# An encoder layer in four passes: the parts of the MLP's weights stored by the first pass, w_down summed over two groups, and POOL's elementwise work moved to VectorE

## The chip, the core and the metric

The kernel runs on one core of one Trainium2 chip. The metric is the device time of one execution in microseconds (us); the median of several executions is compared. The core's engines are named as in the profile: PE is TensorE (the matrix engine, with its weight loads listed apart as PEld), DVE is VectorE, ACT is ScalarE, POOL is GpSimd, and SP is SyncE, whose queue issues most of the DMAs. Each engine takes its instructions in a fixed order and waits by semaphores for the others. SBUF is the memory on the chip in which tiles live, PSUM the eight banks into which PE accumulates.

## What is computed

One layer of a bidirectional encoder on 2048 tokens of width 1024, in float32:

```python
h = x
y = rmsnorm(h, norm_mix_g) @ w_in                     # 1024 -> 2560: q, k, v, conv input and gate
att  = dilated_sliding_attention(rot(q), rot(k), v)   # 8 heads of 64; three window patterns, summed by their softmax weights
conv = silu(layernorm(depthwise_conv31(a * sigmoid(g)) + conv_b))   # 512 channels
h = h + concat([att, conv]) @ w_out                   # 1024 -> 1024
xq = rmsnorm(h, norm_x_g) @ w_xq                      # cross attention: 4 heads of 256, 256 memory rows
h = h + softmax(xq @ xk.T / 16) @ xv @ w_xo
u = rmsnorm(h, norm_mlp_g) @ w_up                     # 1024 -> 4096
h = h + square(relu(u)) @ w_down                      # 4096 -> 1024
out = rmsnorm(h, norm_final_g)
```

## The kernel before

**Numbers in two parts.** PE multiplies float16. Each float32 operand is scaled by a power of two and held as a high part (the value rounded to float16) and a low part (what the rounding left). A product takes three matmuls into the same PSUM tile, high by high, high by low and low by high: `mm3`, lines L369 to L371. A weight tile comes from memory as float32 (`raw`, 512 KB) and is split on the chip by `split_to`: ACT writes the high part (L356) and DVE the low part (L357), each over 128 x 1024 elements.

**Passes.** The front (the projections, the memory's keys and values, the far parts of the attention) takes about the first 680 us. Behind it the tokens are taken in four passes of 512, by `post(p)` (L1464 on): the out-projection (`o`, 8 weight tiles), the cross attention's scores (`xs`, whose weights are the products `ascr` made earlier) and its output (`x`, from `bscr`), the MLP (L1548 to L1586) and the final norm and output (L1589 to L1607). Each of these reads weights through `wpost` (L1322): a DMA of SP into one of three `raw` buffers, then the split into a `ws` buffer. There are four of these, two in the pool `wp` and two in `wq`, and `turn_w` deals them out, two tiles to the one pool and two to the other. So every weight is loaded and split in every pass.

**The MLP of passes 0 to 2.** It runs over eight groups (`fg`) of 512 hidden columns. In a group, four w_up tiles give four PSUM tiles `up` of 24 matmuls of 512 columns each, in the three PSUM banks of kind "mm"; DVE reads each with the norm's scale and the relu (L1564, `rl`), ACT squares and rounds it (L1565, L1566) and DVE takes the low part (L1567). The parts of four tiles (`hh`) lie in a buffer that is one of two (`xquad`). Then four w_down tiles of 256 columns give eight PSUM tiles `dn` of 12 matmuls, and DVE adds each to the residual rows (L1580). The norm's scale comes from a chain that starts where the cross attention ends: PE sums the squares over the partitions (`nps`, L1417), DVE scales (L338, `st_v`), POOL takes the power −1/2 (L342), DVE refines it (L343 to L345), PE spreads it over the partitions (`nrb`, L350), and ACT copies it with a scale (L1545).

**The last pass.** `last_mlp` (L1609) computes its w_down products with seven products where eight stand in the plain form, from sums and differences of quarters of w_down (`quarter`, `sums`) which `piece` splits on the chip (L1691); its `hidden` (L1635) reads w_up through `wpost` as the other passes do.

**Work woven in.** While pass p runs, two generators are advanced by `weave` (L93): the attention of pass p + 1 at 0.95 steps per step of `post`, and its convolution at 0.6. A convolution unit is 31 steps on DVE (L384 and L386, `cacc`); `conv_ln` (L392) norms it over the channels, and at its end POOL scales (L440), ACT rounds (L441) and POOL takes the low part (L442). The attention's inner loop writes scores `s` (L1228), DVE applies the mask and takes the maximum (L1010, `sm`), ACT takes the exponential (L1011), PE transposes (L1017, `pt`), ACT and DVE split (L1020, L1021), PE multiplies by v (L1025 to L1027, `opt`). `combine` (L1121) sums the three patterns of a pair of heads with their softmax weights; its elementwise work is on POOL (`W`), but for the last pair of pass 0.

**What sets the order.** The program is written as these generators. A planner, which simulates the timeline, then fixes each engine's order of instructions; `tc.issue_after` (in `after`) keeps some instructions behind a named one. Tiles of a pool with one tag share buffers, and a new tile waits until the one before it is no longer used.

## Time and profile before

| | |
|---|---|
| median of 3 runs | 2701.1 us (2698.41 to 2701.16) |
| the profiled execution | 2705.9 us |
| its span, first to last instruction | 2704.0 us |
| granted PE clock, mean over the span | 0.994 |
| PE busy | 2645.2 us (98%) |
| DVE busy | 2048.3 us (76%) |
| ACT busy | 1314.5 us (49%) |
| POOL busy | 349.7 us (13%) |
| MLP of pass 0, of pass 1, of pass 2 | 837 to 1209, 1355 to 1726, 1872 to 2241 us |
| DMA | 413.79 MB, mean 153 GB/s |

All rows but the first describe one profiled execution. A row of the timeline reads: start and duration in us, the engine, the line of the kernel, the operation, output <- inputs, shapes, and xN where N like instructions stand in one row; in brackets the idle time of the engine just before it and the instruction that ended it. A row of groups ends with the busy time and the mean ns of one instruction, then the idle time before the group's instructions and what ended most of it. A matmul's recorded duration reaches past the start of the next one, since matmuls are pipelined: the distance of the starts is its cost in a stream. Idle time of an engine that nobody waits for costs nothing.

### The profile page before, as it was taken

The page shows a single profiled execution, that of the slowest core. Times are in us where ns is not written, and L with a number is a line of the kernel's source. Part 1 is how long each engine was busy: PE and PEld are TensorE (multiplying, and loading weights), DVE is VectorE, ACT ScalarE, POOL GpSimd, SP SyncE. Part 2 cuts the span into 40 slices and gives each one's busy share as a digit, 9 for nine tenths or more (in the row PEclk, how much of TensorE's full clock was granted, in tenths as well). Part 3 has the DMA queues.
Part 4 walks back from the last instruction along what each step waited for, and adds up shares of the span by engine and source line. Part 5 has one row for each costly group of instructions (what it writes and reads, how often), then busy time and mean ns, then how long its engine had stood idle before and what let it go on. Part 6 is the DMA issues. An engine that isn't in the chain of part 4 may idle for free.

```text
span 2704.0 us, 41123 instructions
## 1 busy us (share of the span) xinstructions
PE 2645.2 (98%) x15514; PEld 1446.8 (54%) x15514; DVE 2048.3 (76%) x3713; ACT 1314.5 (49%) x2189; POOL 349.7 (13%) x405
## 2 busy tenths in 40 slices
PE   8999999999899999999999999999999999999998
PEld 7844448777454455445545554455445545444443
DVE  5887656567798887667988866689887656679997
ACT  5737554476454344535544344455434434445543
POOL 1144002032001011300011013000110310000000
PEclk9999999999999999999999999999999999999999
DMA  9977968565635444544444545434444445223341
GB/s 270 297 258 215 286 223 266 167 191 163 168 92 134 125 132 124 150 137 150 121 118 124 140 114 164 156 113 125 125 129 129 138 131 179 94 86 102 95 124 63
DMA packets 497702, 413.79 MB, mean 153 GB/s; under 512 B 86525, under 2 KB 432561, under 8 KB 496736
## 3 DMA queue, kind: packets, MB, share of 16 engines
q1 hardware_dynamic: 490096, 396.14, 50.1%
q10 hardware_dynamic: 5184, 9.01, 0.9%
q0 software_dynamic: 2224, 6.01, 0.6%
q8 instruction: 122, 2.00, 0.3%
q14 instruction: 76, 0.62, 0.1%
HBM read 342.52 MB, written 68.57 MB: 152 GB/s over the span
## 4 chain that ended last, share of the span: by engine, by line
PE 79%; DVE 9%; DMA 5%; issue 3%; POOL 2%; ACT 1%; SPq 0%; DVEq 0%; POOLq 0%; ACTq 0%
PE dn L369 7%; PE dn L371 7%; PE dn L370 7%; PE up L369 7%; PE up L370 7%; PE up L371 7%; PE lin L371 3%; PE lin L369 3%; PE lin L370 3%; PE pt L1017 2%; PE xs L369 2%; PE xs L371 2%; PE xs L370 2%; PE o L369 2%; PE o L371 2%
## 5 line engine op out<-in xcount | busy, mean ns | idle before, releaser
L369 PE MATMUL up<-mh,ws_u 128*128 128x512 f16 x1024 | 389.5, 381 | 0.6 <-ACT mh L1457 0.6
L370 PE MATMUL up<-ml,ws_u 128*128 128x512 f16 x1024 | 389.6, 381 | 0.0
L371 PE MATMUL up<-mh,ws_u 128*128 128x512 f16 x1024 | 388.6, 380 | 0.0
L386 DVE SCALAR_TENSOR_TENSOR cacc<-cu,cw,cacc 128x512 f32<-128x512 f32 x480 | 367.6, 766 | 5.0
L371 PE MATMUL dn<-hhh,ws_d 128*128 128x512 f16 x768 | 290.5, 379 | 0.0
L370 PE MATMUL dn<-hhl,ws_d 128*128 128x512 f16 x768 | 290.5, 379 | 0.0
L369 PE MATMUL dn<-hhh,ws_d 128*128 128x512 f16 x768 | 283.1, 379 | 0.9 <-DVE h L1580 0.9
L356 ACT ACTIVATE ws_u<-raw_u,bd 128x1024 f16<-128x1024 f32 x128 | 146.7, 1146 | 237.6 <-PE dn L371 186.9
L356 ACT ACTIVATE ws_d<-raw_d,bd 128x1024 f16<-128x1024 f32 x100 | 114.8, 1148 | 280.2 <-PE up L371 252.4
L1580 DVE SCALAR_TENSOR_TENSOR h<-dn,bd,h 128x512 f32<-128x512 f32 x192 | 140.8, 746 | 62.8 <-PE dn L371 60.1
L357 DVE SCALAR_TENSOR_TENSOR ws_u<-raw_u,bd,ws_u 128x1024 f16<-128x1024 f32 x128 | 164.0, 1282 | 18.5 <-ACT ws_u L356 16.9
L1010 DVE CUSTOM_DVE_ANT_0 sm<-s,mask,qks 128x256 f32<-128x256 f32 (+1 forms) x384 | 150.9, 434 | 29.5 <-PE s L1228 21.6
L371 PEld LDWEIGHTS <-ws_u 128*128 128x128 f16 x1024 | 100.5, 98 | 120.7 <-issue 1.8
L1564 DVE SCALAR_TENSOR_TENSOR rl<-up,ssumx 128x512 f32<-128x512 f32 x96 | 65.7, 690 | 129.5 <-PE up L371 129.3
L369 PEld LDWEIGHTS <-ws_u 128*128 128x128 f16 x1024 | 100.7, 98 | 114.9 <-issue 1.8
L370 PEld LDWEIGHTS <-ws_u 128*128 128x128 f16 x1024 | 101.0, 99 | 113.7 <-issue 1.8
L357 DVE SCALAR_TENSOR_TENSOR ws_d<-raw_d,bd,ws_d 128x1024 f16<-128x1024 f32 x100 | 133.0, 1330 | 30.1 <-ACT ws_d L356 29.5
L1011 ACT ACTIVATE sm<-sm,o 128x256 f32<-128x256 f32 (+1 forms) x288 | 116.3, 453 | 69.9 <-DVE o L1010 69.1
L1021 DVE TENSOR_TENSOR pl<-pt,ph 128x512 f16<-128x512 f32 x160 | 109.4, 685 | 36.5 <-ACT ph L1020 36.3
L371 PEld LDWEIGHTS <-ws_d 128*128 128x128 f16 x768 | 75.1, 98 | 89.2
L1020 ACT CAST ph<-pt 128x512 f16<-128x512 f32 x160 | 91.2, 572 | 60.8 <-PE pt L1017 60.8
L342 POOL TENSOR_TENSOR nr<-st_v,mhalf 128x4 f32<-128x4 f32 (+1 forms) x15 | 13.4, 895 | 825.8 <-DVE st_v L338 825.8
(497 smaller groups left out, 6436.8 us busy)
## 6 DMA issues: line engine op xcount, KB each, us to landing
raw_u<-in_w_up_dram SPq DMA_DIRECT2D x128, 512.0 KB
raw_d<-in_w_down_dram SPq DMA_DIRECT2D x100, 512.0 KB
scan<-in_w_up_dram SPq DMA_DIRECT2D x32, 512.0 KB
scan<-in_w_down_dram SPq DMA_DIRECT2D x32, 512.0 KB
raw_o<-in_w_out_dram SPq DMA_DIRECT2D x32, 512.0 KB
raw_a<-ascr SPq DMA_DIRECT2D x32, 512.0 KB
raw_b<-bscr SPq DMA_DIRECT2D x32, 512.0 KB
b<-in_w_down_dram SPq DMA_DIRECT2D x28, 512.0 KB
```

Of the source, the lines that this page charges most:

```text
L356: ACT.activation(t[:, 0], raw, AF.Copy, scale=scale)
L357: DVE.scalar_tensor_tensor(t[:, 1], raw, scale, t[:, 0], op0=ALU.mult, op1=ALU.subtract)
L369: PE.matmul(o, lh, rh, start=first, stop=False, skip_group_check=more)
L370: PE.matmul(o, lh, rl, start=False, stop=False, skip_group_check=more)
L371: last["pe"] = PE.matmul(o, ll, rh, start=False, stop=end, skip_group_check=more)
L386: DVE.scalar_tensor_tensor(acc, u[:, t:t + 512], cw[:, c, t:t + 1], acc, op0=ALU.mult, op1=ALU.add)
L1010: last["dve"] = DVE.tensor_tensor_reduce(dst, so, mask[:, 256 * m:256 * m + nk], SCORE, 3e38, ALU.add, ALU.min, mn)
L1011: last["act"] = ACT.activation(dst, dst, AF.Exp, bias=mn, scale=-1.0)
L1020: ACT.copy(ph, pt)
L1021: DVE.tensor_tensor(pl, pt, ph, op=ALU.subtract)
L1564: last["dve"] = DVE.scalar_tensor_tensor(r, pt, 0.0, rsb, op0=ALU.max, op1=ALU.mult)
L1580: last["dve"] = DVE.scalar_tensor_tensor(hs[m], pt, K_DN, hs[m], op0=ALU.mult, op1=ALU.add)
```

## The change

It has three parts.

1. **Stored parts.** Pass 0 splits the tiles of w_up and w_down as before and writes both parts of each to a new scratch in memory, `wst`, 64 tiles of 512 KB. A store is issued by `save`, behind the last raw load; `save(1)` leaves the newest split tile unsaved, so that stores run behind, and `save(0)`, called by the first keyed tile of a later pass, stores the rest. In passes 1 to 3 a tile with a `key` is loaded from `wst` straight into a buffer of parts, and nothing is split. Such tiles take turns among seven buffers, the four `ws` and the three `raw` (both have the same size). The keys cover w_up in all passes and w_down in passes 0 to 2; the pieces of the last pass's w_down, and the weights of the other stages, are split as before.
2. **Two groups in PSUM.** In passes 0 to 2 two groups of w_up (eight tiles) are computed ahead of their w_down tiles, and a `dn` PSUM tile sums over both groups, 24 matmuls in place of twice 12. So `hs` is updated 96 times in place of 192. The hidden parts of both groups fill both `xquad` buffers, and the parts of the attention and convolution for the next pass, which used them, go to the buffers of `ct0`, where pass 0's were.
3. **From POOL to DVE.** In `conv_ln` of passes 1 to 3 ACT scales and rounds in one step, and DVE scales and subtracts in one; POOL has none of it. In `combine` of passes 2 and 3 the elementwise work is on DVE.

Counted over the program, DVE goes from 3713 to 3565 instructions, ACT from 2036 to 1876, POOL from 405 to 285, the DMAs issued by SP from 1190 to 1254; the splits go from 397 to 237, and the matmuls stay the same in number and shape.

```diff
...
         return stack.enter_context(tc.tile_pool(name=name, bufs=1, **kw))
     def dma(o, i, q=None):
-        (q or nc.sync).dma_start(o, i)
+        return (q or nc.sync).dma_start(o, i)
     dr = pool("dram", DRAM)
     top = pool("top", side="right")
...
     cath = [dr.tile([P, S], F16, name=f"cath{k}") for k in range(KC)]
     catl = [dr.tile([P, S], F16, name=f"catl{k}") for k in range(KC)]
     gscr = [dr.tile([P, 2, 8, P], F16, name=f"gscr{i}") for i in range(8)]
+    wst = [dr.tile([P, 2 * 1024], F16, name=f"wst{i}") for i in range(64)]
     vscr = dr.tile([P, 2, 8, 256], F16, name="vscr")
     ascr = dr.tile([XH // 2, P, KC, 2 * NMEM], F32, name="ascr")
     bscr = dr.tile([KC, P, KC, P], F32, name="bscr")
...
             ACT.activation(cs[c], cs[c], AF.Silu, bias=gain("ln_b", c), scale=gain("ln_g", c))
         for c in range(4):
             th_, tl_ = [alloc(x, F16, f"l{x}{n}_{c}") if n else cats[0][x[0], 4 + c] for x in ("hi", "lo")]
-            POOL.tensor_scalar(cs[c], cs[c], TC, None, op0=ALU.mult)
-            ACT.copy(th_, cs[c])
-            POOL.tensor_tensor(tl_, cs[c], th_, op=ALU.subtract)
+            if n:
+                ACT.activation(th_, cs[c], AF.Copy, scale=TC)
+                DVE.scalar_tensor_tensor(tl_, cs[c], TC, th_, op0=ALU.mult, op1=ALU.subtract)
+            else:
+                POOL.tensor_scalar(cs[c], cs[c], TC, None, op0=ALU.mult)
+                ACT.copy(th_, cs[c])
+                POOL.tensor_tensor(tl_, cs[c], th_, op=ALU.subtract)
             for t, d in zip((th_, tl_), (cath, catl)) if n else ():
                 dma(d[4 + c][:, sl], t)
             yield
...
         sm_ = top.tile([P, 5, 8], F32, tag="csm", name=f"csm{p}{pr}")
         e3 = top.tile([P, 3, 4, 2], F32, tag="ce", name=f"ce{p}{pr}")
         mm_ = sm_[:, 0].rearrange("p (j h) -> p j h", h=2)
-        W = DVE if end else POOL
+        W = DVE if end or p > 1 else POOL
         with ExitStack() as st:
             after(st, "dve")
             DVE.tensor_tensor(mm_, ld[:, 0, :, :, HD + 1], ld[:, 1, :, :, HD + 1], op=ALU.min)
...
         at = aq.tile([P, 4, 2, HD], F32, tag="cat", name=f"cat{p}{pr}")
         parts = [ld[:, i, :, :, 0:HD] for i in range(2)]
         for i, x in ((2, parts[1]), (0, o0[:, :, :, 0:HD]), (1, parts[0])):
-            (POOL if i == 2 else W).tensor_tensor(x if i else at, x, e3[:, i].unsqueeze(3).to_broadcast([P, 4, 2, HD]),
+            (POOL if i == 2 and p < 2 else W).tensor_tensor(x if i else at, x, e3[:, i].unsqueeze(3).to_broadcast([P, 4, 2, HD]),
                                                   op=ALU.mult)
         for x in parts:
             W.tensor_tensor(at, at, x, op=ALU.add)
...
     turn_w = [0]
-    def wpost(src, name, scale, shape=(P, 8, P)):
+    def wtile(name, n, shape):
+        i = turn_w[0] % n
+        turn_w[0] += 1
+        pl, tag, bufs = (wp, "ws", 2) if i < 2 else (wq, "ws", 2) if i < 4 else (wp, "raw", 3)
+        return pl.tile([P, 2, *shape[1:]], F16, tag=tag, name=f"ws_{name}", bufs=bufs)
+    def flat(t):
+        return t.rearrange("p h a b -> p (h a b)")
+    unsaved = []
+    def save(n):
+        while len(unsaved) > n:
+            key, t = unsaved.pop(0)
+            with ExitStack() as st:
+                after(st, "load")
+                dma(wst[key], flat(t))
+    def wpost(src, name, scale, shape=(P, 8, P), key=None, p=0):
+        if p and key is not None:
+            save(0)
+            t = wtile(name, 7, shape)
+            dma(flat(t), wst[key])
+            return two(t)
         raw = wp.tile(list(shape), F32, tag="raw", name=f"raw_{name}", bufs=3)
-        dma(raw, src)
-        n = turn_w[0]
-        turn_w[0] += 1
-        return two(wsplit2(wq if n % 4 > 1 else wp, raw, name, scale, shape=shape))
+        last["load"] = dma(raw, src)
+        save(1)
+        t = split_to(wtile(name, 4, shape), raw, scale)
+        if key is not None:
+            unsaved.append((key, t))
+        return two(t)
     wout = {}
...
         dma(raw, wcols(w_out, m * P))
         yield
         yield
-        wout[m] = two(wsplit2(wp, raw, f"o0{m}", S_OUT))
-        turn_w[0] += 1
+        t = split_to(wtile(f"o0{m}", 4, (P, 8, P)), raw, S_OUT)
+        wout[m] = two(t)
         yield
     banks.update(mm=(0, 1), S=(3, 4), T=(5, 6), O=(7, 2), c="T")
...
         d = cats.setdefault(p, {})
         for q in "hl":
-            t = xquad(q, half, f"cat{q}{p}{half}")
+            t = ct0.tile([P, 4, 512], F16, tag=f"c{q}{half}", name=f"cat{q}{p}{half}")
             for e in range(4):
                 d[q, 4 * (1 - half) + e] = t[:, e]
         for j in range(2):
...
         if p == NG - 1:
             last_mlp(hs, y, rsb)
             return
-        for fg in range(FG):
+        for g in range(FG // 2):
+            end = g == FG // 2 - 1
             hh = {}
-            for q in "hl":
-                t = xquad(q, fg % 2, f"hh{q}{p}_{fg}")
-                for j in range(4):
-                    hh[q, j] = t[:, j]
-            for c in range(4):
-                wh, wl = wpost(wcols(w_up, fg * 512 + c * P), f"u{p}{fg}_{c}", S_UP)
-                pt = ps("mm", "up")
-                for k in range(KC):
-                    mm3(pt, wh[:, k, :], wl[:, k, :], y["h", k], y["l", k], k == 0, k == KC - 1)
-                r = tmp("rl")
-                last["dve"] = DVE.scalar_tensor_tensor(r, pt, 0.0, rsb, op0=ALU.max, op1=ALU.mult)
-                ACT.activation(r, r, AF.Square)
-                ACT.copy(hh["h", c], r)
-                DVE.tensor_tensor(hh["l", c], r, hh["h", c], op=ALU.subtract)
-                yield
-            if fg == FG - 1:
+            for fg in (2 * g, 2 * g + 1):
+                for q in "hl":
+                    t = xquad(q, fg % 2, f"hh{q}{p}_{fg}")
+                    for j in range(4):
+                        hh[q, 4 * (fg % 2) + j] = t[:, j]
+                for c in range(4):
+                    wh, wl = wpost(wcols(w_up, fg * 512 + c * P), f"u{p}{fg}_{c}", S_UP, (P, 8, P), 4 * fg + c, p)
+                    pt = ps("mm", "up")
+                    for k in range(KC):
+                        mm3(pt, wh[:, k, :], wl[:, k, :], y["h", k], y["l", k], k == 0, k == KC - 1)
+                    r = tmp("rl")
+                    last["dve"] = DVE.scalar_tensor_tensor(r, pt, 0.0, rsb, op0=ALU.max, op1=ALU.mult)
+                    ACT.activation(r, r, AF.Square)
+                    j = 4 * (fg % 2) + c
+                    ACT.copy(hh["h", j], r)
+                    DVE.tensor_tensor(hh["l", j], r, hh["h", j], op=ALU.subtract)
+                    yield
+            if end:
                 fsum = ssum_tile(f"f{p}")
                 load_cat(p + 1, 0)
-            def down(mp2, wh, wl):
+            for mp2 in range(4):
+                ws = [wpost(wcols(w_down, mp2 * 256, 256, (4 * fg, 4 * fg + 4)), f"d{p}{fg}_{mp2}", S_DN, (P, 4, 256),
+                            32 + 4 * fg + mp2, p) for fg in (2 * g, 2 * g + 1)]
                 for e in range(2):
                     m = 2 * mp2 + e
                     es = slice(P * e, P * e + P)
                     pt = ps("mm", "dn")
-                    for k in range(4):
-                        mm3(pt, wh[:, k, es], wl[:, k, es], hh["h", k], hh["l", k], k == 0, k == 3)
+                    for k in range(8):
+                        wh, wl = ws[k // 4]
+                        mm3(pt, wh[:, k % 4, es], wl[:, k % 4, es], hh["h", k], hh["l", k], k == 0, k == 7)
                     last["dve"] = DVE.scalar_tensor_tensor(hs[m], pt, K_DN, hs[m], op0=ALU.mult, op1=ALU.add)
-                    if fg == FG - 1:
+                    if end:
                         add_sq(hs[m], fsum, m == 0)
-            for mp2 in range(4):
-                down(mp2, *wpost(wcols(w_down, mp2 * 256, 256, (4 * fg, 4 * fg + 4)), f"d{p}{fg}_{mp2}", S_DN, (P, 4, 256)))
-                yield
+                    yield
         load_cat(p + 1, 1)
...
         def hidden(fg, c):
-            wh, wl = wpost(wcols(w_up, fg * 512 + c * P), f"u{p}{fg}_{c}", S_UP)
+            wh, wl = wpost(wcols(w_up, fg * 512 + c * P), f"u{p}{fg}_{c}", S_UP, (P, 8, P), 4 * fg + c, p)
             pt = ps("up", "up")
             for k in range(KC):
                 mm3(pt, wh[:, k, :], wl[:, k, :], y["h", k], y["l", k], k == 0, k == KC - 1)
...
             return t
         def piece(w, name):
-            n = turn_w[0]
-            turn_w[0] += 1
-            return two(wsplit2(wq if n % 4 > 1 else wp, w, name, S_DN, shape=(P, 2, 512)))
+            return two(split_to(wtile(name, 4, (P, 2, 512)), w, S_DN))
         def sums(b):
...
```

## Prediction

> **What bounds the kernel now.** I read the page's shares first, then the windows by stage, then the timeline of the one stall that the windows point to, then the groups of instructions that the change takes away. The shares:
>
> ```profile
> span 2704.0 us, 41123 instructions
> ...
> PE 2645.2 (98%) x15514; PEld 1446.8 (54%) x15514; DVE 2048.3 (76%) x3713; ACT 1314.5 (49%) x2189; POOL 349.7 (13%) x405
> ```
>
> TensorE is busy for 98% of the span, and the change leaves its matmuls as they are: the same products of the same sizes, only in another order. So whatever the change takes off the other engines is worth only what it takes out of TensorE's waits, 2704.0 − 2645.2 = 58.8 us in the whole span, and what the clock loses behind them. The windows (each row begins with the window and its length) show what of it lies in the MLP stages of passes 0 and 1, 837 to 1209 and 1355 to 1726 us, and in two short stretches, one in the MLP of pass 1 and one in that of pass 2:
>
> ```profile
> core 0: us, PE busy (x) PEld busy (x) DVE busy (x) ACT busy (x) POOL busy (x), PEclk, DMA share, GB/s
> 1375.00:1385.00 10.00, 7.54 (x38) 3.53 (x35) 10.00 (x22) 6.77 (x13) 3.62 (x5) 0.83 0.66 173
> 1892.00:1902.00 10.00, 7.55 (x39) 3.79 (x37) 10.00 (x21) 6.76 (x13) 3.68 (x5) 0.83 0.64 167
> 837.00:1209.00 372.00, 367.89 (x2034) 184.38 (x2032) 282.84 (x448) 159.37 (x234) 59.66 (x61) 1.00 0.46 129
> 1355.00:1726.00 371.00, 367.89 (x2033) 184.28 (x2032) 283.15 (x447) 159.24 (x233) 59.93 (x61) 1.00 0.46 129
> 0.00:140.00 140.00, 120.14 (x848) 111.27 (x849) 98.28 (x188) 89.55 (x179) 26.40 (x28) 0.99 0.94 286
> ```
>
> TensorE idles 371.00 − 367.89 = 3.1 us of pass 1's MLP, and 10.00 − 7.54 = 2.46 of them lie in the ten microseconds from 1375 on, some 20 us behind the stage's start, where VectorE is busy all the time and the granted clock falls to 0.83. The row of 1892 shows the same in pass 2, as near to its stage's start. The timeline of pass 1's stretch says what it is, first VectorE's (start, duration, instruction), then TensorE's:
>
> ```profile
> 1368.16 1.28 DVE L357 SCALAR_TENSOR_TENSOR ws_d<-raw_d,bd,ws_d 128x1024 f16<-128x1024 f32 x1
> 1369.36 0.16 DVE L338 TENSOR_SCALAR st_v<-nps 128x4 f32<-128x4 f32 x1
> ...
> 1370.97 1.28 DVE L357 SCALAR_TENSOR_TENSOR ws_d<-raw_d,bd,ws_d 128x1024 f16<-128x1024 f32 x1
> 1372.17 0.75 DVE L386 SCALAR_TENSOR_TENSOR cacc<-cu,cw,cacc 128x512 f32<-128x512 f32 x1
> ...
> 1376.42 1.28 DVE L357 SCALAR_TENSOR_TENSOR ws_d<-raw_d,bd,ws_d 128x1024 f16<-128x1024 f32 x1
> ...
> 1379.43 1.88 DVE L1564 SCALAR_TENSOR_TENSOR rl<-up,ssumx 128x512 f32<-128x512 f32 x3
> ```
>
> ```profile
> 1372.62 0.38 PE L369 MATMUL up<-mh,ws_u 128*128 128x512 f16 x1
> 1372.84 0.38 PE L370 MATMUL up<-ml,ws_u 128*128 128x512 f16 x1
> ...
> 1377.02 0.66 PE L1017 MATMUL pt<-ident,sm 128*128 128x128 f32 x4 [0.52 <-ACT ssumx L1545]
> 1378.35 0.20 PE L1025 MATMUL opt<-v,ph 128*128 128x65 f16 x1 [0.68 <-ACT ph L1020]
> ...
> 1379.56 0.27 PE L1228 MATMUL s<-k,qh 128*128 128x256 f16 x1 [0.98 <-DVE low L1010]
> ```
>
> The first three `up` products fill the three PSUM banks of kind "mm". rl (L1564) empties them, and rl needs the norm's scale, which passes down VectorE's queue: st_v, the inverse root, a transposition, ACT's L1545, then rl at 1379.43. In VectorE's queue the low parts of three weight tiles that are needed later (L357, 1.28 each) and steps of the convolution (L386) stand around st_v and ahead of rl. Until rl TensorE lives on scraps of attention and waits 0.52, 0.68 and 0.98. At full clock such products start 0.22 apart (1372.62 to 1372.84).
>
> **The change part by part.** *The splits of passes 1 to 3.* 160 tiles (w_up of passes 1 to 3, 96; w_down of passes 1 and 2, 64) are loaded as parts and no longer split:
>
> ```profile
> L369 PE MATMUL dn<-hhh,ws_d 128*128 128x512 f16 x768 | 283.1, 379 | 0.9 <-DVE h L1580 0.9
> L356 ACT ACTIVATE ws_u<-raw_u,bd 128x1024 f16<-128x1024 f32 x128 | 146.7, 1146 | 237.6 <-PE dn L371 186.9
> L356 ACT ACTIVATE ws_d<-raw_d,bd 128x1024 f16<-128x1024 f32 x100 | 114.8, 1148 | 280.2 <-PE up L371 252.4
> L1580 DVE SCALAR_TENSOR_TENSOR h<-dn,bd,h 128x512 f32<-128x512 f32 x192 | 140.8, 746 | 62.8 <-PE dn L371 60.1
> L357 DVE SCALAR_TENSOR_TENSOR ws_u<-raw_u,bd,ws_u 128x1024 f16<-128x1024 f32 x128 | 164.0, 1282 | 18.5 <-ACT ws_u L356 16.9
> ```
>
> ACT loses 160 × 1.15 = 184 us and VectorE 160 × 1.28 = 205 us. Nearly all of it lies beside a busy TensorE and is worth nothing; what counts is the stall. In the changed order of pass 1, VectorE has between st_v and rl no split, one convolution step, two pl, two low and the norm's own steps, and the attention steps are spread evenly. The norm's chain by its rows:
>
> ```profile
> 1365.33 0.95 PE L1417 MATMUL nps<-ones,ssumx 128*128 128x1 f32 x8
> ...
> 1369.59 1.01 POOL L342 TENSOR_TENSOR nr<-st_v,mhalf 128x4 f32<-128x4 f32 x1 [5.22 <-DVE st_v L338]
> ...
> 1374.21 0.63 PE L350 MATMUL nrb<-ident,nr 128*128 128x128 f32 x4
> ...
> 1376.29 0.67 ACT L1545 ACTIVATE ssumx<-nrb,bd 128x512 f32<-128x512 f32 x1
> ```
>
> Its sums are there at 1365.33 + 0.95 = 1366.3. With st_v at once, 1.0 for the power, four small steps of 0.16, 0.63 and 0.67, some 3 us in all, and up to 3 us of other work between, rl comes at 1369.5 to 1372.5, before the window in which TensorE runs dry. So this stall goes in pass 1, and in pass 2, whose changed order is the same. Pass 0 still splits, its order up to there is unchanged, and whatever stall it has stays. One stall is worth 2.46 us idle and 10 × (1 − 0.83) = 1.7 us of clock, 4.2. The idle is read low: a 512-column matmul is recorded 0.38 long where the next starts 0.22 behind it, 0.16 for each of three or four gaps, at most 5.0. I take 4.8 each, **−9.6** (bounds 0, if something else holds TensorE there, and −10.4, the whole 3.1 idle us of the stage, the 1.7 and 0.4 for the reading).
>
> The clock's part weighs here. The rows show it at 0.83 over stretches in which TensorE was still busy for 7.5 of 10 us, and no gap shown is over 0.98. The Trainium skill ("TensorE: Matmul & The Clock Gate", Part 1: The HAM clock gate) has the clock halve after at least one idle window of some 3.4 us; if that meant a wholly idle window, nothing would be lost to the clock, and the two stalls would be worth 2 × 3.1 = 6.2 in place of 9.6 (an estimate by that page). This trace does not bear that reading out, and I go by its rows.
>
> *Two groups in PSUM.* VectorE's L1580 falls from 192 to 96, 96 × 0.746 = 72 us beside TensorE. TensorE's waits for it were 0.9 us (the row of L369): **−0.9**, bounds 0 and −1.3, the 2 × (3.1 − 2.46) that the two later MLPs idle beside their stalls.
>
> *The convolution's low parts and attention's sums.* VectorE takes from POOL 12 low parts and the sums of 8 pairs of heads, of five 512-column steps and eight small ones each; at 0.75 and 0.16 that is 12 × 0.75 + 8 × 5.0 = 49 us, against 205 + 72 that leave it. In pass 1's MLP it goes from 283 busy us of 371 to 283 − 64 × 1.28 − 32 × 0.75 + 25 = 202. **0**, bounds ±1: one pair's sums can hold VectorE for 5 us, and one `up` tile of 24 matmuls at 0.22, 5.3 us, in a second bank covers them; without that cover a pair costs what is left of its 5 us.
>
> *The stores.* Pass 0's MLP writes 64 × 0.52 MB = 33.6 MB in 372 us, 90 GB/s on top of its 129, in all about 220, where the first 140 us move 286. SP issues a tile's store behind the load of the second tile after it; the store waits for VectorE's split of its tile, and the load queued behind it would have waited for that same split to free its raw buffer. Three raw and four split buffers stand ahead of TensorE. **0**, bounds 0 and +5, one tile late once.
>
> *The last stored tile.* w_down's last tile of pass 0 is stored only when the first stored weight of pass 1 is asked for, behind the out-projection and the whole cross attention. Till then it holds one of the two buffers of pool wq, and nine tiles follow one another through the other. A hand-over needs ACT's and VectorE's part, 1.15 + 1.28 = 2.43 us, beside TensorE's work on the other pool's tiles. In the changed order seven of the nine have 3.3 to 6.3 us of such work (its matmuls at 0.22), but two score tiles (`a103`, `a113`) have 0.87. There TensorE waits 2.43 − 0.87 − 0.44 = 1.1, as two matmuls need the high part alone. **+2.2**, bounds 0.6 (ACT's part alone counts, 1.15 − 0.87) and 4.9 (nothing covers the two).
>
> *Pass 3.* Its w_up parts are loaded into buffers that w_down's split pieces use between; one (the first of group 5) has 2.8 us from the last use of its buffer to its own first use. The nearest load, by SP's issue and ACT's start behind it:
>
> ```profile
> 720.72 0.32 SPq L58 DMA_DIRECT2D raw_a<-ascr  x1
> ...
> 724.29 1.15 ACT L356 ACTIVATE ws_a<-raw_a,bd 128x1024 f16<-128x1024 f32 x1 [1.69 <-DMA raw_a<-ascr]
> ```
>
> 3.57 us: **+0.8**, bounds 0 and +2, if two others with 3.9 and 4.1 come late too.
>
> Sum: −9.6 − 0.9 + 2.2 + 0.8 = **−7.5 us**. The profiled execution took 2705.9, so 2698.4 there; it stands 4.8 above the runs' median, 2701.1, and on that scale the kernel takes **2693.6**.
>
> **The rivals.** *A, slower: the single buffer of pass 1.* VectorE and ACT take splits in their order among the norms' and attention's work. If the hand-overs are late for that reason and not covered, all nine cost 9 × 2.43 = 21.9 in place of 2.2: 2701.1 − 7.5 + 19.7 = 2713. It decides (above 2706.5) from 9.7 + 5.4 = 15.1 us, six to seven of the nine. For it: with one buffer, no split can run ahead, and VectorE is the engine that was late in the stall shown. Against it: seven of nine have 3.3 us or more of other matmuls.
>
> *B, no change: the stall finds another cause.* With the banks full TensorE still has only attention's steps, and those wait for ACT and VectorE in turn (0.68 for ph, 0.98 for low). If the norm's chain is mostly its five hops and not the queue, half of the 9.6 stays: 2693.6 + 4.8 = 2698. Against it: st_v, due at 1366.3, ran at 1369.36, 3.1 us late behind other work of VectorE's queue, and a third split (1376.42) stands just ahead of rl.
>
> *C, slower: the stores hold up the loads.* They stand in SP's one queue ahead of loads. One store of 0.52 MB at 286 GB/s takes 1.8 us; if 1.8 × 64 = 117 us of delay were covered to four fifths only, 23 us would show: 2717. It decides from 12.9 us, a ninth. Against it: the split buffers hold four tiles, some 20 us ahead. The Trainium skill ("DMA: Bandwidth & Descriptors", Issuing engines are not separate DMA queues) says that descriptors of one queue start in order on each DMA engine; no run here shows yet a load behind such a store.
>
> **How the numbers follow.** 0.2%, 5.4 us, is about what a measurement can tell from no change. My forecast, from 2686 to 2695.7, has 0.56. B has 0.24, and some of the forecast's own misses by a microsecond or two are in it. A has 0.13, C 0.07. So faster 0.56, same 0.24, slower 0.20. The range goes from 2686 (every term at its best: −10.4 − 1.3 − 1 + 0.6 = −12.1, and 3 us for small waits elsewhere in passes 1 and 2) to 2709 (A with seven of nine uncovered, 2701.1 − 9.7 + 17.0); above it lie the rest of A and C, 0.15, and below it little.
>
> **What the profile will show.** Right: 20 us behind the start of the MLP in passes 1 and 2 TensorE busy and the clock at 1.00, in pass 0 no change up to there; L1580 at 96 and no L357 for `ws_u` in passes 1 to 3; two waits of about a microsecond for `ws_a` in pass 1. Wrong: a row of waits for `ws_o`, `ws_a`, `ws_b` in pass 1 (A); the clock still at 0.83 early in the MLPs of passes 1 and 2 (B); `up` or `dn` waiting for splits or loads in pass 0 (C), or for the loads of the stored parts later, which I have taken to be ahead.

## The result: 9 us slower, and the profile after

| | before | changed |
|---|---|---|
| median of 9 runs each | 2702.22 us (2698.41 to 2709.86) | 2711.43 us (2708.39 to 2715.56) |
| span of the profiled execution | 2704.0 us | 2712.0 us |
| ratio to before | 1 | 1.003, 95% interval 1.0018 to 1.0042 |

The forecast was 2693.6 us, with 2686 to 2709 as its range: wrong in sign, and the time lies above the range. First the page of the changed kernel: its span, its engines, and two rows of groups (the lines of the changed kernel lie behind those of before by 1 to some 40: L1616 is the L1580 of before, L370 to L372 are `mm3`, L357 and L358 the split).

```profile
span 2712.0 us, 40547 instructions
...
PE 2648.8 (98%) x15514; PEld 1448.3 (53%) x15514; DVE 1833.3 (68%) x3565; ACT 1143.2 (42%) x2029; POOL 224.2 (8%) x285
...
L370 PE MATMUL dn<-hhh,ws_d 128*128 128x512 f16 x768 | 290.8, 379 | 0.0
...
L1616 DVE SCALAR_TENSOR_TENSOR h<-dn,bd,h 128x512 f32<-128x512 f32 x96 | 72.0, 750 | 150.2 <-PE dn L372 149.2
```

The work that was to go from VectorE, ACT and POOL has gone: VectorE is busy 215 us less, ACT 171 us, POOL 125. TensorE's wait for L1616 is 0.0 in place of 0.9. TensorE is busy 3.6 us more, and the span is 8.0 us longer. The windows of the changed kernel say where (window, its length, the busy times of PE, PEld, DVE, ACT and POOL, the granted clock, the DMA share and GB/s): out-projection and cross attention of pass 1; pass 0's MLP; the sixty microseconds from 1090 on in it; pass 1's MLP; pass 2's MLP.

```profile
1215.00:1374.00 159.00, 150.68 (x873) 79.90 (x871) 126.09 (x246) 74.90 (x135) 2.67 (x3) 0.99 0.43 134
837.00:1214.00 377.00, 369.41 (x2018) 183.51 (x2016) 263.62 (x405) 159.14 (x229) 46.10 (x53) 0.99 0.69 214
1090.00:1150.00 60.00, 54.88 (x269) 25.65 (x269) 30.45 (x40) 24.21 (x30) 10.43 (x13) 0.94 0.79 242
1374.00:1737.00 363.00, 362.89 (x2012) 181.71 (x2011) 191.97 (x380) 90.08 (x163) 2.60 (x5) 1.00 0.43 129
1885.00:2249.00 364.00, 364.00 (x2021) 182.75 (x2020) 196.29 (x387) 93.12 (x167) 2.61 (x5) 1.00 0.43 131
```

And two windows of the kernel before that answer to the first and the third of these:

```profile
1209.00:1355.00 146.00, 145.41 (x853) 77.51 (x851) 121.33 (x224) 74.94 (x131) 2.70 (x3) 1.00 0.48 142
...
1090.00:1150.00 60.00, 58.95 (x309) 28.69 (x309) 36.74 (x53) 30.61 (x43) 24.65 (x21) 1.00 0.51 143
```

In the MLPs of passes 1 and 2 TensorE now idles 0.1 and 0.0 us, with the clock at 1.00: the two stalls are gone. But the stages ahead of pass 1's MLP take 159 us in place of 146 (2 of the 13 us are 20 more matmuls of the attention that fall into the stretch), with 159.00 − 150.68 = 8.3 us of idle TensorE, and in the sixty microseconds from 1090 on TensorE idles 5.1 us in place of 1.1.

To sum the waits and the clock together, the next table takes each matmul's start to the next one's, less what such a matmul costs in an undisturbed stream (0.216 us for 512 columns, 0.109 for 256, 0.03 for 64 or 65); what is left is called the gap, and a half clock counts in it. Each column is one profiled execution.

| stage | gaps before | gaps changed | difference |
|---|---|---|---|
| front, up to 680 us | 25.9 | 27.8 | +1.9 |
| pass 0, `o`, `xs`, `x` | 11.2 | 11.2 | 0.0 |
| pass 0, MLP | 8.0 | 14.3 | **+6.3** |
| pass 1, `o`, `xs`, `x` | 1.4 | 12.2 | **+10.8** |
| pass 1, MLP | 7.1 | 1.3 | **−5.8** |
| pass 2, `o`, `xs`, `x` | 1.4 | 1.9 | +0.5 |
| pass 2, MLP | 6.1 | 1.1 | **−5.0** |
| pass 3 | 3.6 | 3.7 | +0.1 |
| sum of the rows | 64.7 | 73.5 | +8.8 |

The front's 1.9 us can't be put down to the change: the front's gaps go from 24.6 to 31.1 over the executions profiled below, whose fronts do the same work. So the gain came as forecast, 10.8 us, and two losses of 17.1 us outweigh it.

**The loss in pass 0** is one wait, before `catT`, the transposition of the sums of the last pair of heads of pass 1's attention. The timeline of the changed kernel, all engines, from the end of that pair's products on:

```profile
1106.83 0.19 PE L1032 MATMUL opt<-v,pl 128*128 128x65 f16 x1
...
1119.35 0.72 ACT L442 ACTIVATE lhi<-lc,bd 128x512 f16<-128x512 f32 x1 [5.60 <-DMA cath<-lhi]
...
1128.47 0.75 DVE L443 SCALAR_TENSOR_TENSOR llo<-lc,bd,lhi 128x512 f16<-128x512 f32 x1 [5.09 <-DMA catl<-llo]
...
1135.68 0.20 DVE L1161 RECIPROCAL csm<-csm 128x8 f32<-128x8 f32 x1
...
1140.79 3.63 POOL L1170 TENSOR_TENSOR cat<-cat,ld 128x512 f32<-128x512 f32 x2
...
1144.47 1.12 PE L1178 MATMUL catT<-ident,cat 128*128 128x128 f32 x4 [5.12 <-POOL cat L1170]
1145.38 0.63 PE L370 MATMUL up<-mh,ws_u 128*128 128x512 f16 x1
1145.81 0.63 PE L371 MATMUL up<-ml,ws_u 128*128 128x512 f16 x1
```

ACT and VectorE stand still for 5.60 and 5.09 us: `lhi` and `llo` share two buffers, and the next tile of the convolution waits until the store of the tile before has landed. The reciprocal of the pair's sum stands behind that, and behind five more instructions, in VectorE's queue, POOL's sums behind the reciprocal, and `catT` behind these; TensorE waits 5.12 us and then runs at half clock (the starts lie 0.43 apart). The row of the kernel before:

```profile
1140.77 0.66 PE L1173 MATMUL catT<-ident,cat 128*128 128x128 f32 x4 [1.05 <-POOL cat L1165]
```

**The loss in pass 1** is a number of waits. TensorE's waits in the changed kernel from 1255 to 1375 us (total, times, longest):

```profile
PE xs L370 <- ACT xp L1525: 2.7, 1, 2.7
PE x L370 <- DVE h L1487: 2.3, 1, 2.3
PE xs L371 <- DVE ws_a L358: 1.1, 2, 0.5
PE xs L370 <- ACT ws_a L357: 0.8, 2, 0.4
PE ptx L1536 <- DVE ptl L1539: 0.6, 1, 0.6
PE s L1233 <- DVE o L1015: 0.6, 1, 0.6
```

Only 1.1 + 0.8 of the 8.1 us are waits for a split. But the wait for the residual (`h`) goes back to the held buffer itself. The next rows are from the queues of SP, ACT, VectorE and TensorE:

```profile
1348.74 0.43 SPq L58 DMA_DIRECT2D wst<-ws_d  x1
...
1358.15 1.15 ACT L357 ACTIVATE ws_b<-raw_b,bd 128x1024 f16<-128x1024 f32 x1 [7.83 <-DMA wst<-ws_d]
...
1359.33 1.28 DVE L358 SCALAR_TENSOR_TENSOR ws_b<-raw_b,bd,ws_b 128x1024 f16<-128x1024 f32 x1 [4.50 <-ACT ws_b L357]
...
1362.52 0.75 DVE L1487 SCALAR_TENSOR_TENSOR h<-x,bd,h 128x512 f32<-128x512 f32 x1
...
1363.32 0.38 PE L370 MATMUL x<-pth,ws_b 128*128 128x512 f16 x1 [2.32 <-DVE h L1487]
```

The store of the held tile is issued at 1348.74. ACT stands still for 7.83 us until it has landed, 9.4 us behind its issue, and only then splits the next tile into the buffer. VectorE's part of that split waits for ACT's, `h` stands behind it in VectorE's queue, and TensorE waits for `h`.

### The profile page after: what moved, and what is told of

Same layout as the page of the kernel before. It is cut to its first block, busy times and chain, and to the rows that moved or that the text cites. A ratio compares the mean times of both kernels' runs of the same rounds, so it can differ in the third digit from the quotient of the medians.

```text
span 2712.0 us, 40547 instructions
## 1 busy us (share of the span) xinstructions
PE 2648.8 (98%) x15514; PEld 1448.3 (53%) x15514; DVE 1833.3 (68%) x3565; ACT 1143.2 (42%) x2029; POOL 224.2 (8%) x285
## 4 chain that ended last, share of the span: by engine, by line
PE 83%; DVE 7%; DMA 5%; issue 2%; ACT 2%; POOL 1%; SPq 0%; DVEq 0%; POOLq 0%; ACTq 0%
PE up L370 8%; PE up L371 8%; PE up L372 8%; PE dn L370 7%; PE dn L371 7%; PE dn L372 7%; PE lin L370 3%; PE lin L372 3%; PE lin L371 3%; PE pt L1022 2%; PE xs L371 2%; PE xs L372 2%; PE xs L370 2%; PE o L370 2%; PE o L372 2%
## 5 line engine op out<-in xcount | busy, mean ns | idle before, releaser
L370 PE MATMUL up<-mh,ws_u 128*128 128x512 f16 x1024 | 389.6, 381 | 0.6 <-DMA ws_u<-wst 0.5
L372 PE MATMUL up<-mh,ws_u 128*128 128x512 f16 x1024 | 389.0, 380 | 0.0
L370 PE MATMUL dn<-hhh,ws_d 128*128 128x512 f16 x768 | 290.8, 379 | 0.0
L372 PE MATMUL dn<-hhh,ws_d 128*128 128x512 f16 x768 | 290.7, 379 | 0.0
L1616 DVE SCALAR_TENSOR_TENSOR h<-dn,bd,h 128x512 f32<-128x512 f32 x96 | 72.0, 750 | 150.2 <-PE dn L372 149.2
L372 PEld LDWEIGHTS <-ws_u 128*128 128x128 f16 x1024 | 100.5, 98 | 121.3 <-issue 2.1
L370 PEld LDWEIGHTS <-ws_u 128*128 128x128 f16 x1024 | 100.8, 98 | 113.9 <-issue 1.9
L1598 ACT ACTIVATE rl<-rl 128x512 f32<-128x512 f32 x96 | 60.2, 628 | 169.8 <-DVE rl L1597 169.7
L372 PEld LDWEIGHTS <-ws_d 128*128 128x128 f16 x768 | 75.1, 98 | 90.0
L370 PEld LDWEIGHTS <-ws_d 128*128 128x128 f16 x768 | 75.3, 98 | 83.3
L371 PEld LDWEIGHTS <-ws_d 128*128 128x128 f16 x768 | 75.1, 98 | 83.5
L1022 PE MATMUL pt<-ident,sm 128*128 128x128 f32 x640 | 97.5, 275 | 6.0 <-ACT sm L1016 3.3
L372 PE MATMUL o<-cath,ws_o 128*128 128x512 f16 x256 | 97.7, 383 | 5.2 <-DVE ws_o L358 5.2
```

Source lines behind the costliest of these rows:

```text
L370: PE.matmul(o, lh, rh, start=first, stop=False, skip_group_check=more)
L371: PE.matmul(o, lh, rl, start=False, stop=False, skip_group_check=more)
L372: last["pe"] = PE.matmul(o, ll, rh, start=False, stop=end, skip_group_check=more)
L1022: last["pe"] = PE.transpose(pt[:, j, :], sm[:, j, :], ident)
L1598: ACT.activation(r, r, AF.Square)
L1616: last["dve"] = DVE.scalar_tensor_tensor(hs[m], pt, K_DN, hs[m], op0=ALU.mult, op1=ALU.add)
```

## The experiments

The ratios are to runs of the kernel before on the same chip, with 95% intervals; the gaps are counted as in the table above.

### The held buffer of pass 1

```diff
-        save(1)
+        save(1 if key is not None else 0)
         t = split_to(wtile(name, 4, shape), raw, scale)
```

> The changed kernel, but every store that is due is issued as soon as a weight of another stage is loaded, so that both buffers of pool wq are free from pass 1's out-projection on. Theory (the held buffer cost what pass 1's scores and output lost): the waits of xs and x in pass 1, start to start 12.1 us with their clock, fall back to the 1.3 of before, so the time falls by some 10.5 to 11 us, to about 0.999 of before; the stall before catT at 1139 stays at 5 us. Rival (the scores' waits come from another order of VectorE's work and not from the buffer): they stay, and the time stays within 3 us of the changed kernel's.

Measured: 0.9984 (0.9975 to 0.9994), faster than before and some 12 us faster than the changed kernel. The gaps of `o`, `xs` and `x` in pass 1 are 1.4, as before. The windows of this run, the three stages and then the two MLPs behind them:

```profile
1208.00:1356.00 148.00, 147.41 (x873) 79.50 (x871) 126.02 (x242) 74.30 (x133) 3.17 (x3) 1.00 0.45 140
1356.00:1720.00 364.00, 363.85 (x2019) 182.43 (x2017) 191.93 (x384) 90.92 (x165) 2.61 (x5) 1.00 0.44 128
1869.00:2233.00 364.00, 363.43 (x2017) 182.37 (x2016) 196.34 (x387) 93.11 (x167) 2.60 (x5) 1.00 0.45 131
```

All of pass 1's loss hangs on the held buffer: not only the waits for a split, but also those for the softmax (`xp`) and for the residual (`h`). The latter is the wait for the held tile's store that the rows above show. For the softmax no row leads to the buffer; in the two traces the engines' orders in this stage differ (the planner lays the attention's and the convolution's work otherwise when there is one buffer), and that this order made the wait is likely, not shown. The rival, another order of VectorE's work without the buffer, falls. Before `catT` TensorE still waited, 2.7 us where 5 were expected.

### The convolution's parts back on POOL

```diff
-            if n:
-                ACT.activation(th_, cs[c], AF.Copy, scale=TC)
-                DVE.scalar_tensor_tensor(tl_, cs[c], TC, th_, op0=ALU.mult, op1=ALU.subtract)
-            else:
-                POOL.tensor_scalar(cs[c], cs[c], TC, None, op0=ALU.mult)
-                ACT.copy(th_, cs[c])
-                POOL.tensor_tensor(tl_, cs[c], th_, op=ALU.subtract)
+            POOL.tensor_scalar(cs[c], cs[c], TC, None, op0=ALU.mult)
+            ACT.copy(th_, cs[c])
+            POOL.tensor_tensor(tl_, cs[c], th_, op=ALU.subtract)
```

> The changed kernel with the convolution's scaling and low parts on POOL again in all passes. Theory (in VectorE's and ACT's queues the low and high parts wait for the store of the tile before and hold up the reciprocal of the pair's sum and the splits behind it): the 5.1 us wait before catT at 1139 and the half clock behind it go, some 6.5 us, to about 1.0005 to 1.001 of before; the waits of xs and x in pass 1 stay. Rival (the stores in SP's queue delay the loads of w_up and with them the whole of VectorE): a wait of 3 us or more stays before catT or goes to up.

Measured: 1.0035 (1.0024 to 1.0047), no better than the changed kernel, and TensorE's wait before `catT` is as long:

```profile
PE catT L1174 <- POOL cat L1166: 5.4, 1, 5.4
```

Together with the early store:

> Both at once: the early store of the first run and the convolution's parts on POOL as in the second. If the two losses are separate, their gains add to some 17 us from the changed kernel: about 2694, 0.997 of before, as the stalls at the start of the MLP in passes 1 and 2 stay away. If one of them only covered the other, it ends at 2700 or more.

Measured: 0.9987 (0.9978 to 0.9996), no gain over the early store alone, with gaps of 14.3 us in pass 0's MLP. And the step alone, on the kernel before:

> The kernel before with this one step of the change: the convolution's high parts scaled on ACT and its low parts on VectorE in passes 1 to 3; no stored weights, no pairs of groups. Theory (the wait for the store of the tile before is enough by itself): a wait of 2 us or more before catT in pass 0's MLP, where the kernel before has 1.1, and 2 to 6 us more time. Rival (it needs the new stores in the same queue): catT's wait stays under 1.5 us, and the time is within 2 us of before.

Measured: 1.0007 (0.9997 to 1.0016), no difference that shows, and before `catT`:

```profile
PE catT L1177 <- POOL cat L1169: 0.8, 1, 0.8
```

My first theory of the loss in pass 0 fell with these three. On POOL the parts of the convolution wait for the same landings, and POOL's sums stand behind them there: it is the same chain on another engine.

### The loads of the next pass's parts, and the stores

The loads of `load_cat` now go to free buffers, so SP issues them a few places behind the stores of the same rows (in the changed kernel `cath<-lhi` at 1114.35 and the load `cath<-cath` at 1119.33). This run (on the early store) puts them behind the last raw load:

```diff
             if end:
                 fsum = ssum_tile(f"f{p}")
-                load_cat(p + 1, 0)
...
-        load_cat(p + 1, 1)
+        with ExitStack() as st:
+            after(st, "load")
+            load_cat(p + 1, 0)
+            load_cat(p + 1, 1)
```

> The first run's kernel (early store), with the loads of the next pass's attention and convolution parts (load_cat) put behind the last load of a w_down tile; in pass 0 SP then issues them in one piece at the end of the MLP. Theory S (in SP's queue each of these loads stands a few places behind the store of the same rows and waits for it to land; the convolution's next stores and the weights' loads queue up behind that wait, and with them the tiles of the convolution, the reciprocal and the pair's sum): the waits of lhi and llo for their own stores shrink to the kernel before's 6 us or less in sum, catT's wait in pass 0 to about 1, the gaps of pass 0's MLP from 10.6 to about 8: 0.9970 to 0.9978 of before. Rival W (the stores of the weights in the same queue and the same DMA engines make the small stores slow): the waits and the 2.7 us before catT stay.

Measured: 0.9979 (0.9969 to 0.9988), the same as the early store alone. Theory S falls: `catT` waited, and longer than the 2.7 us of rival W:

```profile
PE catT L1178 <- POOL cat L1170: 4.9, 1, 4.9
```

The pairs of groups alone, on the kernel before: the MLP loop and `load_cat` of the change, `wpost` without keys.

> The kernel before with the second part alone: pairs of groups in PSUM, hence the next pass's parts in the buffers of pass 0's, where their loads are free to go early; all weights split as before, nothing stored, POOL's work left on POOL. Theory S: a wait of 2 us or more before catT in pass 0's MLP, and of lhi and llo for DMAs of more than 8 us, without any store of weights. Rival W: catT's wait is about 1 as before. Both: the stalls at the start of the MLP of passes 1 and 2 stay (gaps of 5 to 6 us there); the time is within 5 us of before, above it by theory S.

Measured: 1.0035 (1.0024 to 1.0047), 9.9 us above before by the medians where 5 were expected at most. `catT` waited in pass 0, without any stored weight, and the stalls at the start of the MLPs of passes 1 and 2 stayed (gaps of 12.1 and 5.2 us, with a second wait before `catT`, 4.2 us in pass 1, among the 12.1):

```profile
PE catT L1173 <- POOL cat L1165: 5.0, 1, 5.0
```

The stored weights with a group at a time (keys in the loop of before, `load_cat` in `xquad`'s buffers, the early store; the third part stays in):

> The first run's kernel (stored parts, early store, VectorE for POOL) without the second part: groups one by one and the next pass's parts in xquad's buffers as before, so their loads come late. Theory S: catT's wait is about 1 in pass 0 although the weights are stored; the stalls at the start of the MLP in passes 1 and 2 are away; some 0.5 us for dn in each of the passes: 0.9970 to 0.9980 of before. Rival W: catT waits 2.5 us or more and pass 0's MLP has gaps of 10 us or more, 0.9984 or above.

Measured: 0.9983 (0.9973 to 0.9992). The stalls of passes 1 and 2 are away (gaps 1.7 and 1.4); `catT` waited here too:

```profile
PE catT L1178 <- POOL cat L1170: 4.2, 1, 4.2
```

So neither the early loads nor the stores are needed for the wait: with one of them away the rest of the change still gave it. The pairs alone bring it, and the stored weights with the third part bring it without pairs. What these runs share is seen when the chain is measured against TensorE's work. The start of the pair's last product, of the last matmul ahead of `catT` (plus 0.22), and of `catT` give two lengths in each trace: the matmuls that stand between, and the time that the chain took.

| run, pass 0 | matmuls between, us | chain, us | wait, us |
|---|---|---|---|
| before | 34.5 | 35.7 | 1.2 |
| convolution's step alone | 34.8 | 35.7 | 0.9 |
| changed | 32.4 | 37.6 | 5.3 |
| convolution's parts on POOL | 33.3 | 38.9 | 5.6 |
| the same, early store | 33.3 | 39.6 | 6.3 |
| early store | 32.2 | 35.1 | 2.8 |
| late loads, early store | 32.2 | 37.3 | 5.1 |
| the same, third part undone (below) | 32.4 | 37.2 | 4.7 |
| pairs alone | 32.2 | 37.4 | 5.1 |
| stored, no pairs | 34.8 | 39.2 | 4.4 |

In the kernel before the chain was already longer than the matmuls ahead of it, by 1.2 us. With pairs of groups 1.2 to 2.3 us less of TensorE's work stands between. With pairs, stored weights or both the chain is 1.5 to 3.9 us longer, but for the early store's one profile, in which it is 0.6 us shorter. In passes 1 and 2 the changed kernel has 31.6 us between and waits for nothing.

### More room ahead of the transposition

```diff
         for x in parts:
             W.tensor_tensor(at, at, x, op=ALU.add)
         yield
         yield
+        for _ in range(2 if p == 1 and pr == H // 2 - 1 else 0):
+            yield
```

On the early store:

> The first run's kernel (early store) and two more steps between the sums and the transposition of the last pair of heads of pass 1's attention (woven into pass 0), so that TensorE has some 5 to 11 us more of matmuls ahead of it. Theory L (the wait before catT is a chain of latencies of 35 to 39 us, from the pair's last product through the convolution's end and the sums, against 32 us of matmuls that the order leaves between; the pairs of groups shortened the latter from 34.5, loads and stores of the changed pass 0 lengthened the former from 35.7): the work between becomes 38 us or more, the wait goes to under 0.5 us with its half clock, the gaps of pass 0's MLP fall to 5 to 6, the time to 0.9965 to 0.9975 of before. Rival Q (VectorE's and ACT's queues are late as a whole in that stretch, so any later place waits as well): the wait stays above 2 us, or goes to up.

Measured: 2692.17 us against 2703.73, **0.9958 (0.9942 to 0.9974)**. The matmuls between are 47.1 us, nothing waits before `catT`, and the gaps of pass 0's MLP are 4.2. The windows of this run, pass 0's MLP and the sixty microseconds that held the wait:

```profile
834.00:1200.00 366.00, 363.58 (x2014) 181.68 (x2012) 262.24 (x404) 157.95 (x227) 46.10 (x53) 1.00 0.71 221
1090.00:1150.00 60.00, 60.00 (x305) 28.04 (x301) 32.86 (x40) 28.39 (x35) 9.42 (x12) 1.00 0.79 250
```

The DMA share there is 0.79 as in the changed kernel, and VectorE runs 40 instructions there in both: what the edit moves is the place of the transposition. The rival, engines late as a whole, falls. This version beats both kernels; its 11.6 us under before are near the 10.5 us of gain that were forecast without the losses. On the changed kernel, without the early store:

> The changed kernel with the two steps alone, the stores left as they are. Theory L: pass 0's MLP loses its wait as in the run with both, the waits of xs and x in pass 1 (gaps 7.3 and 4.8) stay: some 6 us under the changed kernel, 1.0003 to 1.0015 of before; the two losses add. Rival Q: as the changed kernel, 1.003.

Measured: 0.9992 (0.9982 to 1.0002). Pass 0's MLP has gaps of 5.9 us, 8.4 fewer than in the changed kernel, and `o`, `xs` and `x` of pass 1 keep their 12.2: the two losses are separate. The time is some 10 us under the changed kernel's, where 6 were expected.

### What the parts are worth, and a control

The third part undone on the run with late loads (`W = DVE if end else POOL`, POOL for the product with `i == 2`, and the convolution as in the second experiment):

> The kernel of late loads and early store with the third part undone: the convolution's parts and the pair's sums on POOL in all passes. If VectorE, freed of the splits, has room for both, the third part is worth nothing (within 2 us of the run with late loads). If POOL's slower sums (1.3 to 1.4 us a step) come late for catT somewhere in passes 1 and 2, it is up to 3 us slower; if VectorE's queue was hurt by the sums, it is faster.

Measured: 0.9997 (0.9984 to 1.001) against 0.9979 (0.9969 to 0.9988) with it. The intervals overlap, so this settles no more than that the moves to VectorE did no harm; in pass 1 a wait of 1.7 us before `catT` shows in its gaps, which the run with VectorE's sums doesn't have.

A group at a time, with early store and room:

> The version with early store and two more steps, without the pairs of groups (a group at a time, as before). It prices the second part by itself, beside the other two with both losses mended. By the rows of before the pairs are worth 0.9 us: this run then stands within 2 us of the version with pairs, 0.9955 to 0.9970 of before, with the waits of dn for L1580 back (0.5 us a pass). If the pairs were worth nothing but the shorter way to catT, it is the same or faster.

Measured: 0.9969 (0.9956 to 0.9982), 0.9958 with pairs: the pairs may be worth some 3 us once `catT` has room, but the intervals overlap.

The room alone, on the kernel before:

> The kernel before with the two more steps alone. In it the wait before catT is 1.2 us and no half clock follows, so the steps are worth 1 us at most: 0.999 to 1.0005 of before. If they were worth 5 us or more here too, the gain of the version with both would not be the change's.

Measured: 1.0 (0.999 to 1.001). On the kernel before, whose wait there is 1.2 us, the two steps are worth nothing that shows; the gain of the best version is the change's own.

## Why the prediction was wrong, step by step

- *The stall of passes 1 and 2, −9.6, and the waits for L1580, −0.9.* Right in mechanism and size: the gaps of the two MLPs fell by 5.8 + 5.0 = 10.8, 10.5 forecast. The norm's chain in the changed kernel's pass 1, from the sums to rl:

```profile
1379.78 1.05 PE L1448 MATMUL nps<-ones,ssumx 128*128 128x1 f32 x8
...
1388.53 1.28 DVE L1597 SCALAR_TENSOR_TENSOR rl<-up,ssumx 128x512 f32<-128x512 f32 x2
```

  It takes 1388.53 − 1380.83 = 7.7 us where it took 1379.43 − 1366.28 = 13.1; I had bounded it at 3 to 6. That was short enough: the stage's gaps are 1.3 us in all, and rival B, a stall of another cause, didn't come.
- *The clock's part.* The two stalls were worth 10.8 us by the gaps, idle time and clock together. The reading of the Trainium skill ("TensorE: Matmul & The Clock Gate", Part 1: The HAM clock gate) by whole idle windows would have given 6.2, an estimate by that page, and the gaps do not agree with it. The changed kernel's trace shows the half clock behind one unbroken wait of 5.12 us, the run with the early store behind one of 2.69.
- *The last stored tile, +2.2.* The step that failed first, by its size: 10.8 us. I had counted the two hand-overs that the split itself delays, and these came as worked out, at the fourth and the eighth of the score tiles (1.1 + 0.8 us of waits in the view, 2.5 us as gaps). But I took the rest of the stage to cost nothing, and it didn't: TensorE waited 2.7 us for the softmax, ran at half clock behind that, and waited 2.3 us for the residual. A term for the last hand-over, which waits not for a split but for the held tile's store to land (9.4 us from its issue), was missing from the sum. The early store removes all of it. Rival A named the place and the buffer; its price, 21.9 us, was twice too high.
- *The stores, 0, and the pairs, which I costed only by their L1580.* The step that failed outright. I looked for loads that come late, and TensorE waited for none in pass 0's MLP; the view of its waits there begins with 5.1 us before `catT`. What came late was a chain of latencies through the convolution's small stores, two buffers, VectorE's queue and POOL's sums, which was uncovered by 1.2 us in the kernel before already. A row of the groups of before had shown it, POOL's idle 15.1 us behind the stores of `llo`, and I did not ask who stands behind it:

```profile
L442 POOL TENSOR_TENSOR llo<-lc,lhi 128x512 f16<-128x512 f32 x12 | 18.9, 1576 | 15.1 <-DMA catl<-llo 15.1
```

  The pairs took 2 us of TensorE's work out of the way, the chain grew by 1.9 us, and the wait and its half clock cost 6.3 us. Rival C named the stores in SP's queue, and the convolution's small stores stand there too; but the victim was not a load, and the wait comes without any stored weight as well. What rival C takes from the Trainium skill stands in the next section of that page ("DMA: Bandwidth & Descriptors"), Two DMAs through the same engine are not ordered.
- *The convolution's parts and the sums, 0.* Nothing measurable by themselves: 1.0007 for the convolution's step on the kernel before; on the changed kernel the intervals with and without overlap.
- *Pass 3, +0.8.* The pass's gaps grew by 0.1. TensorE waited 0.5 us in all for stored parts there, twice; in the run with late loads it was 1.0, in the one with early store and room 0.7, so the size was of the order forecast.

How much of the chain's 1.9 us more is due to the stores and how much to the loads behind them is open: each run has one profile, and the early store alone shows 35.1, with the late loads 37.3, which nothing in the edit explains, and the pairs alone, without any stored weight, show 37.4.

## What to carry to other kernels

Where one engine is busy for 98%, ask of each chain of latencies that ends in its queue how much of its work stands between the chain's start and its end: once the chain is the longer of the two, as it was here by 1.2 us, a change that shortens this work, or lengthens the chain by 2 us, costs the difference in full, with the clock on top if TensorE runs at half clock behind it, although every single cost lies beside other work. A buffer that is held across a stage "until it is convenient" can cost more than the hand-overs that you count (10.8 us against 2.2 here): the tile that needs it at the end waits for the store to land, and the work around it may be ordered otherwise. Release it at the first chance. And a row in which an idle engine waits for a store to land is a sign of a chain, not of a free engine: look up who is behind it.

## What was not expected of the hardware

The granted clock answered to single waits of quite different lengths: it fell to half behind 5.12 us (changed kernel, window 1144 to 1150, clock 0.50, the first row below) and behind 2.69 us (run with the early store, the starts 0.43 apart for some 3.4 us), while a wait of 1.79 us that ended at 679.68 left it at 1.00 (second row).

```profile
1144.00:1150.00 6.00, 5.53 (x15) 2.52 (x16) 2.85 (x3) 1.82 (x3) 0.42 (x1) 0.50 0.81 222
...
677.00:684.00 7.00, 5.21 (x45) 3.43 (x44) 3.47 (x9) 2.61 (x6) 1.43 (x2) 1.00 0.98 219
```

And the store of a 128 KB tile, issued into a DMA share of 0.79, held its buffer for 5.0 and 6.3 us (`cath<-lhi` issued at 1114.35, ACT's next step free at 1119.35; `catl<-llo` issued at 1122.13, VectorE's at 1128.47), some ten times what its bytes take at the 242 GB/s of that window, 0.5 us.
